# A two-layer backbone on one core: the order of one step's loads, of a gate and of some norms, two free PSUM banks, and a merged store

## The chip, the cores and the metric

The kernel runs on one core of one Trainium2 chip. A core has five engines that run side by side and wait for each other through semaphores: TensorE (PE in the profile, its weight loads PEld), VectorE (DVE), ScalarE (ACT), GpSimd (POOL) and SyncE (SP), which here only issues DMA transfers. Matmul results land in PSUM, which has eight banks; everything else lives in SBUF or in the chip's memory. The metric is the device time of one execution in microseconds; lower is better.

## The reference

Two layers work on 512 latent tokens and 256 context tokens of width 1024. Layer 0 is a bidirectional gated DeltaNet with 16 value heads, layer 1 is attention with 8 query heads, 2 key heads and an axial rotary. Each layer ends in a gate (SiLU) and an output projection, and the output is an RMS norm of the latent stream.

```python
def step(s, xs):                                   # layer 0, one chunk of 64 tokens
    qk_i, qd_i, kd_i, u_i, w_i, gl_i = xs
    v_new = u_i - jnp.einsum('bhcd,bhde->bhce', w_i, s)
    o = jnp.einsum('bhcd,bhde->bhce', qd_i, s) + jnp.einsum('bhcs,bhse->bhce', qk_i, v_new)
    s = s * gl_i[..., None, None] + jnp.einsum('bhcd,bhce->bhde', kd_i, v_new)
    return s, o

def finish(o, z):                                  # layer 0, after both directions
    o = rms_norm(jnp.transpose(o, (0, 2, 1, 3)), o_norm_g)
    return (o.reshape(b, l, DN_VAL_DIM) * jax.nn.silu(z)) @ w_out

def gqa_attend(q, k, v):                           # layer 1, q and k normed and rotated
    s = jnp.einsum('bqhgd,bkhd->bhgqk', qg, k).astype(F32) * (d ** -0.5)
    p = jax.nn.softmax(s, axis=-1)
    return jnp.einsum('bhgqk,bkhd->bqhgd', p, v).reshape(b, lq, hq, d)

h_lat = h_lat + gate[:, None] * y_lat              # each layer
return rms_norm(h_lat, final_norm_g)               # the end
```

## The kernel before

Tokens lie in six tiles of 128 rows: tiles 0 and 1 hold the context, 2 to 5 the latents. A tile pairs a chunk of 64 tokens from the front with one from the back, so that the forward and the backward direction are worked at once, one in each half of the partitions. Large products are made in three passes (`PASS`: high times high, high times low, low times high), for which operands are split into a high part, a cast by ScalarE, and a low part, a subtraction by VectorE or GpSimd.

**Up to 537 us** the projections, convolutions and the chunk matrices of layer 0 are computed, in an order that a planner in the code writes out; keys, queries, values, T (the inverted triangle) and QK of each tile are stored to memory. The last products of this part are `pp` and `pw` (L837, L861), the last store is that of T of tile 5 (L852).

**The recurrence (L1761 to L1800)** has 12 steps of 4 groups, `x` from 0 to 47, in a loop `for x in range(50)` with a pipeline of three stages: `products(x)` (state times keys and queries into `ks`, L1562; VectorE's `r`, L1565; ScalarE's `o`, L1568; GpSimd's scaling of the state, L1571, and on a second visit its sum O + o, L1574), `solve(x-1)` (T times r into `pr_all` or `pq_all`, L1588; its copy `vn`, L1590; the scaled copy `vd`, L1598 or L1600) and `update(x-2)` (QK times vn, L1614; keys times vd into `su`, L1622; VectorE's additions to O, L1628, and to the state, L1634 and L1636). Step 0 starts from a zero state and skips `products`. The two PSUM tiles `pr_all` and `pq_all` alternate with x; one half takes the solve, the other the QK product, so the solve of a group waits until the addition (L1628) of the group two before it has read its tile.

`load_step(s)` issues the loads of a step when its first group begins: key `ck` and query `cq` (L1534), two halves of the values `cv` (L1010), T (L1002), QK (L1003) and the turned key `ckt` (L1004), all on SyncE's queue. A queue issues in order; a load whose buffer is still in use holds all behind it.

At the end of the recurrence the output part of layer 0 starts for its first heads: `out_scale` (ScalarE), `out_turn` (transposes into `pt`, L1699), `out_gated` (VectorE, L1708), `out_cast` (the high half, ScalarE, L1715), `out_rest` (the low half, VectorE, L1721), then `out_product` (L1742). This order is written by hand for TensorE, VectorE, ScalarE and GpSimd.

**Layer 1** is written by hand too. Before the loop over `u` (32 pairs of a head and a tile, four more turns to drain) keys and the first queries are normed and rotated: `k_rotated` (L2086, L2087, GpSimd's sum L2088), `k_turned`, `q_cosines` and `q_sines` (L2172 to L2180), and `q_norm_steps` (L2192 to L2200), eleven small VectorE instructions of Newton steps, of which `some(norms, n)` runs the next n. In step u: `scores(u)` (L2233) into `s3`, `maxima(u)` (L2239, L2241), the exponential in `powers(u)` (ScalarE, L2248), transposes of step u-2 (L2261), products with the values (L2282) into the left half of the bank `po`, and up to u = 23 a piece of the query and gate projections (L2162, L2213). The maxima lie in `spare`, the right half of that bank. From u = 26 on `out_block` (L2296) fills the place of the pieces.

**The tail** takes the last projection of tiles 2 and 3 in chunks of columns (`CHUNKS`): tile 3 has one of 512 and two of 256, of which the last two lie in the two halves of `po`. `finish_part` (L2448 to L2450) gates a chunk, adds it and squares it, `finish_norm` takes the root, and `send` stores each half of a tile by a DMA of its own (L2471).

Of the kernel before, what the change touches and what calls it, by code (L numbers as in the profile page):

```python
# [12 lines left out]
ALU = mybir.AluOpType  # L13
# [4 lines left out]
P = 128  # L18
# [68 lines left out]
def backbone(tc, a, out):  # L87
    nc = tc.nc
    V, S, G, T = nc.vector, nc.scalar, nc.gpsimd, nc.tensor
    dma = nc.sync.dma_start  # L90
# [1039 lines left out]
    last = {}  # L1130
# [373 lines left out]
    if True:  # L1504
# [11 lines left out]
        def load_step(s):  # L1516
            nm = f"_{s}"
            t, visit = where(s)
            if s == 0:
                (Tt, QK, kt), v = opening["m"], opening["v"]  # L1520
                loads[s] = (None, kt, v, Tt, QK)
                return
            if s % 2:
                Tt = ch.tile([P, VH, 64], F32, tag="T", name="cT" + nm, bufs=1)
                v = ch.tile([P, VH, P], F32, tag="v", name="cv" + nm, bufs=1)
                QK = ch.tile([P, VH, 64], F32, tag="QK", name="cQK" + nm, bufs=1)
                kt = ch.tile([P, QH, P], F32, tag="kt", name="ckt" + nm, bufs=1)
            k0 = ch.tile([P, QH, P], F32, tag="kq0", name="ck" + nm, bufs=1) if s % 2 else by_key_heads(even_tile(s, "k"))
            if not s % 2:
                Tt, QK = even_tile(s, "T"), even_tile(s, "QK")  # L1530
                kt, v = by_key_heads(even_tile(s, "kt")), values_tile(s)
            kq = [k0, ch.tile([P, QH, P], F32, tag="kq1", name="cq" + nm)]
            for w, src in enumerate((k_d, q_d)):
                dma(kq[w], src[t])  # L1534
            values_loaded(t, v)
            mark[0] = matrices_loaded(t, visit, Tt, QK, kt)
            loads[s] = (kq, kt, v, Tt, QK)


# [37 lines left out]
        def solve(x):  # L1577

            s, p = divmod(x, 4)
            t, visit = where(s)  # L1580
            Tt = loads[s][3]
            r, = live[x]
            pr_ = prq[x % 2][:, :, 0:2]
            for i in range(2):
                for j in range(2):
                    for hf in range(2):
                        r0, o0 = hf * 64, (hf ^ j) * 64
                        T.matmul(pr_[o0:o0 + 64, j, i], Tt[r0:r0 + 64, 4 * p + 2 * j + i, :], r[r0:r0 + 64, 2 * j + i], start=True, stop=True)  # L1588
            vn = ch.tile([P, 4, P], F32, tag="vn", name=f"vn{x}", bufs=2)
            (V.tensor_copy if x == 0 else S.copy)(vn.rearrange("p (j i) d -> p j i d", j=2), pr_)  # L1590
            vd = None
            if s < 11:
                vd = ch.tile([P, 4, P], F32, tag="vd", name=f"vd{x}", bufs=2)
                for c in range(4):
                    h = 4 * p + c
                    el = (elX if c > 1 else elV)[:, visit, t, h:h + 1]
                    if s == 0 and p < 2:
                        V.tensor_scalar(vd[:, c], vn[:, c], el, None, ALU.mult)  # L1598
                    else:
                        S.activation(vd[:, c], vn[:, c], AF.Copy, scale=el)  # L1600
            live[x] = [vn, vd]
# [151 lines left out]
    AB, C = (0, 1), (2,)  # L1753
    squares = [(t, h) for t in (1, 0, 5) for h in range(VH)]
    for x in range(50):
        if x < 48:
            products(x)
        if x == 45:
            out_scale(0, AB)
        if x == 46:  # L1760
            out_scale(0, C)  # L1761
        if 0 <= x - 1 < 48:
            solve(x - 1)
        if x == 47:
            out_gated(0)
            out_cast(0)
            out_rest(0)
        if 0 <= x - 2 < 48:
            update(x - 2)
        if x == 45:  # L1770
            psU_c.__exit__(None, None, None)
            psV_c = tc.tile_pool(name="psV", bufs=2, space=PSUM, reuse_waits="tile")
            turning["p"] = psV_c.__enter__()
        if 14 <= x < 30 or x >= 35:
            for t, h in squares[:2]:
                square_o(t, h)
            del squares[:2]
        if x == 1:
            V.tensor_tensor(or2, rq, rq, ALU.mult)
        if 30 <= x < 42:  # L1780
            some(ctx_chain, (2, 4, 1, 1, 1, 1, 1, 1, 1, 1, 1, 99)[x - 30])
        if x in (43, 44, 45):
            some(chain, (3, 7, 99)[x - 43])
        if x in (28, 32, 36, 40):
            with tc.issue_after(mark[0]):
                (out_load if x < 36 else gate_load)((x - 28) // 4 % 2)
        if x in (44, 45):
            out_high(x - 44)
        if x == 46:
            out_low(0)  # L1790
            out_turn(0)
        if x == 47:
            out_low(1)
            out_load(2)
        if x == 48:
            out_scale(1)
            out_product(0, 0)
            out_turn(1)
# [436 lines left out]
    def maxima(u):  # L2235
        hq, t = divmod(u, 4)
        b = u % 2
        top = spare[:, b:b + 1]
        V.tensor_reduce(top, s3[:, b], AX.X, ALU.max, negate=True)  # L2239
        nm_ = at.tile([P, 1], F32, tag="nm", name=f"nm{u}")  # L2240
        V.tensor_tensor(nm_, top, qTs["s", hq // 2][:, t, hq % 2:hq % 2 + 1], ALU.mult)  # L2241
        return nm_
# [77 lines left out]
    some(norms, 5)  # L2320
    q2 = q_cosines(0, 2)
    q_sines(0, 2, q2)
    some(norms, 99)
    z_products(1, range(4))
    q_turned(0, 1, qo)
    k_turned(4, kr.pop(4))
    kr[5] = k_rotated(5)
    z_products(1, range(4, 8))
    q_turned(0, 2, q2)
    kv_values(lat)  # L2330
# [22 lines left out]
    for u in range(32 + 4):  # L2353
# [12 lines left out]
        elif last and u % 2 == 0:  # L2366
            z_tanh(last[1])
        if u == 0:
            q_sines(*last[1:], o)
            norms = q_norm_steps(0, spare[:, 16:48], 3, 4)  # L2370
        if turning:
            turn(u - 2, ps)
            turned(u - 2, ps)
        nm_ = maxima(u) if u < 32 else None
        if o is not None and u:
            q_sines(*last[1:], o)
        if turning:
            turned_lo(u - 2, ps)
# [3 lines left out]
            powers(u, nm_)  # L2382
        if u % 8 == 6 and u < 24:
            norms = q_norm_steps(u // 8 + 1, pg[0][:, 256:288], 0, 4)
        if u % 8 in (6, 7) or u == 0:
            some(norms, 7 if u % 8 == 6 else 99)
        for half in range(2):
            if piece and piece[0] is q_products:
# [42 lines left out]
    gated(15)  # L2431


    acc = [pg, acc1, [tr_tile(f"pso2{nh}").rearrange("p a b -> p (a b)") for nh in range(2)], [s_all[:, 1024:1536], po]]

    jks = [f2.tile([P, D], F32, tag="jko", name=f"jko{t}") for t in range(2)]
    CHUNKS = [((0, 512), (512, 512))] * 3 + [((0, 512), (512, 256), (768, 256))]

    def out_chunk(k, t, c0, n):
        cc_, (bank, b0) = slice(c0, c0 + n), divmod(c0, 512)  # L2440
        for x, (i, j) in enumerate(PASS):
            T.matmul(acc[t][bank][:, b0:b0 + n], yT[i][:, k, t * P:(t + 1) * P], wo[j][:, k, cc_], start=k == 0 and x == 0, stop=k == KT - 1 and x == 2)

    def finish_part(t, i):
        c0, n = CHUNKS[t][i]
        c, (bank, b0) = slice(c0, c0 + n), divmod(c0, 512)
        jk = jks[t]
        V.tensor_tensor(jk[:, c], acc[t][bank][:, b0:b0 + n], gate1[:, 0, c], ALU.mult)  # L2448
        V.tensor_tensor(hs[t][:, c], hs[t][:, c], jk[:, c], ALU.add)
# [16 lines left out]
        return y  # L2466

    def send(t, x, c, q):
        for hf in range(2):
            c_ = t if hf == 0 else 7 - t  # L2470
            q(out[0, c_ * 64:c_ * 64 + 64, c], x[hf * 64:hf * 64 + 64, c])  # L2471
# [99 lines left out]
```

## Time and profile before

| what | value |
|---|---|
| median of 3 runs | 1148.21 us (1148.09 to 1150.12) |
| the profiled execution | 1148.87 us |
| its span, first to last instruction | 1147.0 us |
| mean granted TensorE clock | 0.995 |
| ScalarE busy | 749.1 us (65%) |
| VectorE busy | 787.8 us (69%) |
| GpSimd busy | 600.9 us (52%) |

Times in the profile are microseconds from the start of the span. An engine's busy time is counted by instruction; an engine that is idle waits for a semaphore, and the profile names the engine, line and tile whose end came last before it went on. TensorE's matmuls are pipelined, so the rows of two neighbours overlap, and an end of a group is a little later than the start of the next. "SPq" and "ACTq" are the sequencers that issue DMA transfers; the row of an issue says nothing of when the data is there, for which the list of DMA issues has a landing time.

### The profile page before, as it was taken

The page shows a single profiled execution, that of the slowest core. Times are in us where ns is not written, and L with a number is a line of the kernel's source. Part 1 is how long each engine was busy: PE and PEld are TensorE (multiplying, and loading weights), DVE is VectorE, ACT ScalarE, POOL GpSimd, SP SyncE. Part 2 cuts the span into 40 slices and gives each one's busy share as a digit, 9 for nine tenths or more (in the row PEclk, how much of TensorE's full clock was granted, in tenths as well). Part 3 has the DMA queues.
Part 4 walks back from the last instruction along what each step waited for, and adds up shares of the span by engine and source line. Part 5 has one row for each costly group of instructions (what it writes and reads, how often), then busy time and mean ns, then how long its engine had stood idle before and what let it go on. Part 6 is the DMA issues. An engine that isn't in the chain of part 4 may idle for free.

```text
span 1147.0 us, 27235 instructions
## 1 busy us (share of the span) xinstructions
PE 1108.2 (97%) x10511; PEld 904.6 (79%) x10511; DVE 787.8 (69%) x1628; ACT 749.1 (65%) x1998; POOL 600.9 (52%) x521
## 2 busy tenths in 40 slices
PE   5999999999999999998999999999999999999996
PEld 2777788888888888887566665888787889999885
DVE  4786656688899978783688877355546476667646
ACT  4554554477877888675789888875767356666731
POOL 0554111239999999940675688556645253130900
PEclk9999999999999999999999999999999999999999
DMA  9589744765748886756998983686844112001323
GB/s 367 199 287 326 261 143 130 226 178 166 232 128 241 264 246 205 207 181 193 291 258 244 276 252 101 196 224 184 239 136 138 55 57 63 30 19 56 111 74 92
DMA packets 117138, 208.69 MB, mean 182 GB/s; under 512 B 12145, under 2 KB 76818, under 8 KB 111762
## 3 DMA queue, kind: packets, MB, share of 16 engines
q1 hardware_dynamic: 97074, 195.32, 55.2%
q10 hardware_dynamic: 19936, 11.64, 3.4%
q8 instruction: 83, 1.36, 0.5%
q14 instruction: 45, 0.37, 0.1%
HBM read 166.16 MB, written 40.67 MB: 180 GB/s over the span
## 4 chain that ended last, share of the span: by engine, by line
PE 89%; DVE 3%; issue 2%; DMA 2%; ACT 2%; POOL 1%; SPq 0%; POOLq 0%; ACTq 0%; DVEq 0%
PE g_v L926 12%; PE g_z L926 12%; PE po L1742 9%; PE ks L1562 7%; PE g_k L500 6%; PE g_q L926 6%; PE pg L2162 4%; PE su L1622 3%; PE pg L2213 3%; PE po L2282 3%; PE s L2233 3%; PE kv L2044 2%; PE pa L316 2%; PE pt L2261 2%; PE pq_all L1588 1%
## 5 line engine op out<-in xcount | busy, mean ns | idle before, releaser
L1742 PE MATMUL po<-woh,y 128*128 128x512 f32 x384 | 129.2, 401 | 0.0
L1571 POOL TENSOR_TENSOR S<-S,glb 128x512 f32<-128x512 f32 x80 | 81.9, 1045 | 82.3 <-PE ks L1562 82.1
L1680 POOL TENSOR_TENSOR wol<-wo,woh 128x1024 fp32r<-128x1024 f32 x32 | 77.5, 2422 | 55.9 <-ACT woh L1673 54.2
L810 POOL TENSOR_TENSOR X<-X,tmp 128x62 f32<-128x62 f32 (+15 forms) x93 | 98.6, 1060 | 7.3
L809 POOL TENSOR_TENSOR tmp<-L,X 128x62 f32<-128x62 f32 (+15 forms) x93 | 91.9, 989 | 6.7
L926 PE MATMUL g_z<-uh,wh_z 128*128 128x512 f32 (+1 forms) x256 | 88.6, 346 | 0.0
L926 PE MATMUL g_v<-uh,wh_v 128*128 128x512 f32 (+1 forms) x256 | 88.0, 344 | 0.0
L941 DVE SCALAR_TENSOR_TENSOR acc_v<-g_v,cwv,acc_v 128x510 f32<-128x510 f32 (+3 forms) x128 | 77.7, 614 | 14.5 <-ACT acc_v L933 11.0
L926 PE MATMUL g_z<-ul,wh_z 128*128 128x512 f32 (+1 forms) x256 | 86.9, 339 | 0.4 <-issue 0.4
L926 PE MATMUL g_z<-uh,wl_z 128*128 128x512 f32 (+1 forms) x256 | 86.6, 338 | 0.0
L926 PE MATMUL g_v<-ul,wh_v 128*128 128x512 f32 (+1 forms) x256 | 86.1, 336 | 0.0
L926 PE MATMUL g_v<-uh,wl_v 128*128 128x512 f32 (+1 forms) x256 | 86.1, 336 | 0.0
L1742 PEld LDWEIGHTS po<-woh,y 128*128 128x128 f32 x384 | 72.3, 188 | 15.4 <-issue 0.3
L1742 PE MATMUL po<-wol,y 128*128 128x512 f32 x192 | 75.4, 393 | 0.0
L1636 DVE TENSOR_TENSOR S<-su,S 128x512 f32<-128x512 f32 x80 | 51.5, 686 | 8.1 <-PE su L1622 6.5
L1708 DVE SCALAR_TENSOR_TENSOR pt<-pt,og,z 128x128 f32<-128x128 f32 x96 | 34.4, 358 | 32.5 <-PE pt L1699 30.2
L555 POOL TENSOR_TENSOR kt<-kt,kss 128x768 f32<-128x768 f32 x8 | 11.6, 1472 | 85.6 <-DVE kss L183 57.1
L1562 PE MATMUL ks<-S,ck 128*64 128x256 f32 x352 | 55.4, 392 | 1.0 <-ACT O L1568 1.0
L1565 DVE SCALAR_TENSOR_TENSOR r<-ks,negV,cv 128x128 f32<-128x128 f32 x176 | 52.3, 344 | 5.2 <-PE ks L1562 2.2
L1562 PE MATMUL ks<-S,cq 128*64 128x256 f32 x352 | 53.6, 379 | 0.0
L926 PEld LDWEIGHTS g_z<-ul,wh_z 128*128 128x128 f32 x256 | 49.0, 191 | 5.4 <-issue 0.6
L926 PEld LDWEIGHTS g_z<-uh,wl_z 128*128 128x128 f32 x256 | 48.9, 191 | 5.4
(463 smaller groups left out, 3341.6 us busy)
## 6 DMA issues: line engine op xcount, KB each, us to landing
aw<-in_ada_late SPq DMA_DIRECT2D x16, 1024.0 KB, 7.3
wo<-in_dn_w_out SPq DMA_DIRECT2D x32, 512.0 KB, 3.7
cv<-v_d SPq DMA_DIRECT2D x22, 512.0 KB, 8.7
aw<-in_ada_first SPq DMA_DIRECT2D x8, 1024.0 KB, 11.6
w_z<-in_dn_w_in SPq DMA_DIRECT2D x16, 512.0 KB, 5.0
w_v<-in_dn_w_in SPq DMA_DIRECT2D x16, 512.0 KB, 4.5
v_d<-vt ACTq DMA_DIRECT2D x16, 384.0 KB, 4.2
cT<-t_d SPq DMA_DIRECT2D x12, 512.0 KB, 9.4
```

Source lines behind the costliest of these rows:

```text
L500: T.matmul(kbank[h, i][:, :n], w[:, k], u[:, k, c0:c0 + n], start=k == 0 and n_ == 0, stop=k == KT - 1 and n_ == len(passes) - 1)
L809: G.tensor_tensor(tv, bcast(L[:, :, j + 1:, j], 3, j + 1), bcast(X[:, :, j, 0:j + 1], 2, n), ALU.mult)
L810: G.tensor_tensor(X[:, :, j + 1:, 0:j + 1], X[:, :, j + 1:, 0:j + 1], tv, ALU.subtract)
L926: T.matmul(ps[:, :m], w[:, k], u[:, k, c0:c0 + m], start=k == 0 and n_ == 0, stop=k == KT - 1 and n_ == 2)
L941: V.scalar_tensor_tensor(acc[:, c0 + lo:c0 + hi], ps[:, lo + j - 2:hi + j - 2], cwv[:, j, ct:ct + 1], acc[:, c0 + lo:c0 + hi], ALU.mult, A ...
L1562: T.matmul(ks[r0:r0 + 64, w], kq[w][:, hh, r0:r0 + 64], St[hh][:, d], start=True, stop=True)
L1565: V.scalar_tensor_tensor(r[:, 2 * j + i], ks[:, 0, i], negV[:, visit, t, h:h + 1], v[:, h], ALU.mult, ALU.add)
L1571: G.tensor_tensor(St[hh], St[hh], bcast(g_, 3, P), ALU.mult)
L1636: V.tensor_tensor(St[hh], sj, St[hh], ALU.add)
L1680: G.tensor_tensor(wl, raws.pop(n), halves[n][0], ALU.subtract)
L1742: T.matmul(acc[nh], y[i][:, j, :], ww[k][:, nh * 512:(nh + 1) * 512], start=h == 0 and x == 0, stop=h == VH - 1 and x == 2)
L2162: T.matmul(q_bank(p, t), uL[i][:, k, t * P:(t + 1) * P], wq[j][:, k], start=k == 0 and n_ == 0, stop=k == KT - 1 and n_ == 2)
```

## The change

Seven places change.

1. `load_step`: in step 1 the query is loaded behind values, T and QK, ahead of the turned key. Other steps keep their order.
2. `solve`: in step 0 the scaled copies `vd` of groups 2 and 3 are made by GpSimd, two instructions of two heads each, in place of four on ScalarE.
3. The loop of the recurrence, at x = 47: `out_gated(0)` and `out_cast(0)` stand ahead of `products(47)`, `out_rest(0)` behind `update(45)`; before, all three stood between `solve(46)` and `update(45)`.
4. `maxima`: in steps 24 and 25 the result lies in `pg[0]`, a bank that no product uses in those steps, in place of `spare`.
5. Ahead of the loop over u, the last Newton steps stand behind `k_turned(4)` and `k_rotated(5)`.
6. In the loop, at u = 0, `q_sines` stands behind `maxima(0)` as in other steps, and the Newton steps of the last query tile run at u = 1 in place of u = 0.
7. The tail: the last chunk of tile 3 lies in `pg[0]`, and tile 3, whose two halves are neighbours in the output, is stored by one DMA for each column half in place of two.

```diff
             kq = [k0, ch.tile([P, QH, P], F32, tag="kq1", name="cq" + nm)]
-            for w, src in enumerate((k_d, q_d)):
-                dma(kq[w], src[t])
+            dma(kq[0], k_d[t])
+            if s > 1:
+                dma(kq[1], q_d[t])
             values_loaded(t, v)
-            mark[0] = matrices_loaded(t, visit, Tt, QK, kt)
+            dma(Tt, t_d[t, :, visit])
+            dma(QK, qk_d[t, :, visit])
+            if s == 1:
+                dma(kq[1], q_d[t])
+            mark[0] = dma(kt, kt_d[t]).ins
...
-                    if s == 0 and p < 2:
+                    if s == 0 and p > 1:
+                        if c % 2 == 0:
+                            G.tensor_tensor(vd[:, c:c + 2], vn[:, c:c + 2], bcast((elX if c > 1 else elV)[:, visit, t, h:h + 2], 2, P), ALU.mult)
+                    elif s == 0:
                         V.tensor_scalar(vd[:, c], vn[:, c], el, None, ALU.mult)
...
     for x in range(50):
+        if x == 47:
+            out_gated(0)
+            out_cast(0)
         if x < 48:
             products(x)
...
             solve(x - 1)
-        if x == 47:
-            out_gated(0)
-            out_cast(0)
-            out_rest(0)
         if 0 <= x - 2 < 48:
             update(x - 2)
+        if x == 47:
+            out_rest(0)
...
-        top = spare[:, b:b + 1]
+        top = (pg[0] if u in (24, 25) else spare)[:, b:b + 1]
...
-    some(norms, 99)
     z_products(1, range(4))
     q_turned(0, 1, qo)
     k_turned(4, kr.pop(4))
     kr[5] = k_rotated(5)
+    some(norms, 99)
     z_products(1, range(4, 8))
...
         if u == 0:
-            q_sines(*last[1:], o)
             norms = q_norm_steps(0, spare[:, 16:48], 3, 4)
...
-        if o is not None and u:
+        if o is not None:
             q_sines(*last[1:], o)
...
-        if u % 8 in (6, 7) or u == 0:
+        if u % 8 in (6, 7) or u == 1:
             some(norms, 7 if u % 8 == 6 else 99)
...
-    acc = [pg, acc1, [tr_tile(f"pso2{nh}").rearrange("p a b -> p (a b)") for nh in range(2)], [s_all[:, 1024:1536], po]]
+    acc = [pg, acc1, [tr_tile(f"pso2{nh}").rearrange("p a b -> p (a b)") for nh in range(2)], [s_all[:, 1024:1536], po, pg[0]]]
...
+    def place(t, c0):
+        return (2, 0) if t == 3 and c0 == 768 else divmod(c0, 512)
...
     def send(t, x, c, q):
+        if t == 3:
+            q(out[0, 192:320, c], x[:, c])
+            return
         for hf in range(2):
```

More of the change, by code (lines that the diff above doesn't have):

```diff
@@ L2431, in backbone @@
     gated(15)
-    acc = [pg, acc1, [tr_tile(f"pso2{nh}").rearrange("p a b -> p (a b)") for nh in range(2)], [s_all[:, 1024:1536], po]]
+    acc = [pg, acc1, [tr_tile(f"pso2{nh}").rearrange("p a b -> p (a b)") for nh in range(2)], [s_all[:, 1024:1536], po, pg[0]]]
     jks = [f2.tile([P, D], F32, tag="jko", name=f"jko{t}") for t in range(2)]
     CHUNKS = [((0, 512), (512, 512))] * 3 + [((0, 512), (512, 256), (768, 256))]
+    def place(t, c0):
+        return (2, 0) if t == 3 and c0 == 768 else divmod(c0, 512)
     def out_chunk(k, t, c0, n):
-        cc_, (bank, b0) = slice(c0, c0 + n), divmod(c0, 512)
+        cc_, (bank, b0) = slice(c0, c0 + n), place(t, c0)
         for x, (i, j) in enumerate(PASS):
@@ L2445, in finish_part @@
         c0, n = CHUNKS[t][i]
-        c, (bank, b0) = slice(c0, c0 + n), divmod(c0, 512)
+        c, (bank, b0) = slice(c0, c0 + n), place(t, c0)
         jk = jks[t]
```

## The prediction

> **What bounds the kernel now.** I read the page first, then the waits of TensorE alone, then, at each wait that the change touches, the timeline and the chain of waits. The page:
>
> ```profile
> span 1147.0 us, 27235 instructions
> PE 1108.2 (97%) x10511; PEld 904.6 (79%) x10511; DVE 787.8 (69%) x1628; ACT 749.1 (65%) x1998; POOL 600.9 (52%) x521
> ```
>
> TensorE is busy 97% of the span, and the change takes no matmul away. 1147.0 - 1108.2 leaves 38.8 us, so it can gain only where TensorE waits and at the two ends. The list of TensorE's waits has six that the change touches, none above 2.5 us; each is shown below. Between them TensorE is full, as a window of the recurrence shows (us, then busy us of TensorE, its weight loads, VectorE, ScalarE, POOL, each with its count, then granted clock, DMA share, GB/s):
>
> ```profile
> 553.00:644.00 91.00, 91.00 (x1540) 58.87 (x1536) 73.88 (x168) 80.05 (x276) 59.30 (x56) 1.00 0.93 261
> ```
>
> So a microsecond won at one place arrives at the end. The DMA engines are at 0.93 there, but loads are issued as TensorE frees buffers, so an earlier TensorE also means earlier loads.
>
> **Part 1: step 1's loads.** From the timeline (start, us, engine, line, operation; in brackets the idle time before it and what ended it); the sixth row is from SyncE's waits (us, times, longest):
>
> ```profile
> 526.25 0.33 SPq L1534 DMA_DIRECT2D ck<-k_d  x1
> 534.85 0.32 SPq L1534 DMA_DIRECT2D cq<-q_d  x1
> 535.22 2.37 SPq L1010 DMA_DIRECT2D cv<-v_d  x2
> 543.65 1.29 DVE L1634 COPY S<-su 128x512 f32<-128x512 f32 x2 [1.31 <-PE su L1622]
> 546.93 0.61 DVE L1565 SCALAR_TENSOR_TENSOR r<-ks,negV,cv 128x128 f32<-128x128 f32 x2 [1.99 <-DMA cv<-v_d]
> SPq L1534 <- PE pw L861: 8.2, 1, 8.2
> 543.99 0.60 PE L1562 MATMUL ks<-S,cq 128*64 128x256 f32 x4
> 548.31 0.65 PE L1562 MATMUL ks<-S,ck 128*64 128x256 f32 x4 [0.96 <-ACT O L1568]
> 551.08 0.67 PE L1588 MATMUL pr_all<-r,cT 64*64 64x128 f32 x16 [0.83 <-ACT O L1626]
> ```
>
> The query load (cq) waits 8.2 us for the last `pw` product, with values, T and QK behind it in SyncE's queue. The values come so late that r starts at 546.93, though VectorE was free at 543.65 + 1.29 = 544.94. With the query behind them, the three can go out right after the key, from 526.6 on. Then r starts 1.99 earlier, and what follows it on ScalarE does too. What is late next is TensorE itself: without the 0.96, the second ks group starts at 547.35; it takes 1.94 (548.31 to 551.08 - 0.83) and ends at 549.29, when the copy that pr_all waits for is done since 551.08 - 1.99 = 549.09. Both waits go: 0.96 + 0.83 = **1.8 us**.
>
> The new risk is the query, used at 543.99 and now behind 2 MB. The load on the DMA engines, the two ends of the old order (landing time at the end of the row) and ScalarE's 1 MB store of T:
>
> ```profile
> 525.00:535.00 10.00, 9.81 (x254) 7.99 (x255) 0.69 (x1) 4.14 (x8) 0.00 (x0) 0.83 0.62 214
> 535.00:545.00 10.00, 9.03 (x150) 6.89 (x150) 5.31 (x15) 6.01 (x13) 0.26 (x1) 1.00 0.87 267
> cq<-q_d SPq DMA_DIRECT2D x1, 512.0 KB, 3.9
> cQK<-qk_d SPq DMA_DIRECT2D x1, 512.0 KB, 12.8
> 537.18 0.34 ACTq L852 DMA_DIRECT2D t_d<-Tt  x1
> ```
>
> From 525 to 535 the queues moved 10 x 214 = 2.14 MB; the moved loads add 2.0, the query 0.5: 4.64 MB, which at 267 GB/s are through at 525 + 17.4 = 542.4, in time. If the whole store of 537.18 goes first, 1 MB or 3.8 us come on top: 546.2, and TensorE waits 2.2. I take "in time", since the values can start eight microseconds sooner, and keep 1.8 - 2.2 = -0.4 to 1.8 as bounds. [...]
>
> In step 0, groups 2 and 3 now scale vd on POOL, in two instructions for ScalarE's four. The trace has none such; the nearest has its size (ns, shortest, median, longest), and POOL is idle until its first scaling of S:
>
> ```profile
> L2088 POOL TENSOR_TENSOR kr<-kr,tmk x4: 732/735/741, 911.2 to 925.7; 128x256 f32<-128x256 f32 x4
> 544.74 2.04 POOL L1571 TENSOR_TENSOR S<-S,glb 128x512 f32<-128x512 f32 x2 [42.72 <-PE ks L1562]
> ```
>
> 2 x 0.735 = 1.5 us. Group 3 follows that scaling and its own vn (near 547.3), so it is ready near 548.8; its su comes after pr_all and the QK product, near 550.3. **0 us**, covered by those 1.5; if the cover were gone, at most 1.5 lost, and nothing gained, as ScalarE is not late there.
>
> **Part 2: the first head gated ahead.** The end of the recurrence:
>
> ```profile
> 710.64 0.33 PE L1699 MATMUL pt<-ident,so 128*128 128x128 f32 x1 [0.32 <-ACT so L1692]
> 712.03 0.61 DVE L1565 SCALAR_TENSOR_TENSOR r<-ks,negV,cv 128x128 f32<-128x128 f32 x2 [1.22 <-PE ks L1562]
> 713.26 0.62 PE L1614 MATMUL pq_all<-vn,cQK 64*64 64x128 f32 x16
> 713.42 1.14 DVE L1708 SCALAR_TENSOR_TENSOR pt<-pt,og,z 128x128 f32<-128x128 f32 x3
> 715.59 0.68 DVE L1628 TENSOR_TENSOR O<-pq_all,O 128x512 f32<-128x512 f32 x1
> 716.32 0.67 PE L1588 MATMUL pq_all<-r,cT 64*64 64x128 f32 x16 [2.44 <-DVE O L1628]
> ```
>
> TensorE waits 2.44 for the addition of group 45 (L1628), which VectorE does behind the gating (1.14), the wait for ScalarE's cast and the low half. The change puts gating and cast before the products of group 47, the low half behind the addition. The gating can start at 710.64 + 0.33 = 710.97, ends near 712.15 in VectorE's idle 1.22, and delays r by 0.1. The addition then waits for its product only, 713.26 + 0.62 and 0.1 of passage: 714.0 in place of 715.59, **1.6 us**. The low half follows at 714.7, before the first projection can start (near 715.8). Bounds: 1.0 (r and ScalarE's o pushed by the cast) to 2.4.
>
> **Part 3: norms.** TensorE's wait for the rotation of key 5, the last Newton step that stands before it, and the first steps of the attention loop:
>
> ```profile
> 923.63 0.17 DVE L2200 SCALAR_TENSOR_TENSOR sq<-kv,qy 128x6 f32<-128x6 f32 x1
> 926.45 0.44 PE L2070 MATMUL kt<-ident,kr 128*128 128x128 f32 x2 [0.34 <-POOL kr L2088]
> 932.60 1.33 PE L2233 MATMUL s<-kT,qT 128*128 128x512 f32 x6 [0.25 <-ACT pr L2248]
> 932.66 0.15 DVE L2192 TENSOR_SCALAR po<-sq 128x2 f32<-128x2 f32 x1
> 934.64 0.16 DVE L2200 SCALAR_TENSOR_TENSOR sq<-po,qy 128x2 f32<-128x2 f32 x1
> 937.19 0.19 ACT L2248 ACTIVATION_READ_ACCUMULATOR pr<-s,nm,sq 128x1 f32 x1
> 937.43 1.31 PE L2233 MATMUL s<-kT,qT 128*128 128x512 f32 x6 [0.75 <-ACT pr L2248]
> ```
>
> Six steps of 0.2 us, the last at 923.63, move behind that rotation: 1.2 earlier, and the 0.34 goes, **0.3 us** (0 to 0.34). At u = 0 the sines (two instructions, some 0.8) move behind the first maxima, and eleven steps, 932.66 to 934.80, behind the second exponential. Scores of step u start 0.05 after the exponential of u-1 is read out (937.19 + 0.19 = 937.38, 937.43). Both exponentials come earlier, by 0.8 and about 1.3, more than the waits: 0.25 + 0.75 = **1.0 us** (0.25 to 1.0). Late next are the third maxima, pushed by the moved steps to some 938.3; their exponential would end near 940.6, before TensorE is through its 2.9 us of query products.
>
> **Part 4: maxima of steps 24 and 25 in a free bank.** The value products no longer wait for them:
>
> ```profile
> 1064.08 1.32 PE L2282 MATMUL po<-pT,vv 128*128 128x256 f32 x9 [0.93 <-DVE nm L2241]
> 1064.95 0.19 ACT L2248 ACTIVATION_READ_ACCUMULATOR pr<-s,nm,sq 128x1 f32 x1
> 1067.77 1.32 PE L2282 MATMUL po<-pT,vv 128*128 128x256 f32 x9 [0.60 <-DVE nm L2241]
> 1068.65 0.19 ACT L2248 ACTIVATION_READ_ACCUMULATOR pr<-s,nm,sq 128x1 f32 x1
> ```
>
> The waits sum to 1.53. But the order seen in part 3 is late next: the scores follow the exponential. Exponential 24 is read out at 1065.14, so scores 25 start at 1065.19 at the earliest; now the value products end at 1065.40. That wins 0.2, and 0.2 again one step later (1068.89 against 1069.09): **0.4 us**, bounds 0 and 1.5.
>
> **Part 5: the tail.**
>
> ```profile
> 1130.39 5.83 PE L2442 MATMUL po<-wo,yT 128*128 128x256 f32 x48
> 1136.26 0.42 DVE L2448 TENSOR_TENSOR jko<-po,gate 128x256 f32<-128x256 f32 x1 [2.39 <-PE po L2442]
> 1137.85 0.41 DVE L2448 TENSOR_TENSOR jko<-po,gate 128x256 f32<-128x256 f32 x1
> L2471 ACTq DMA_DIRECT2D out<-hg x2: 562/584/605, 1142.2 to 1142.8; - x2
> ```
>
> The second chunk is complete after 24 of the 48 matmuls, near 1133.4, but its reading waits for all, as the third lies in its bank. With the third elsewhere, the second's work is over by 1135.6, and the third's starts at 1136.26 in place of 1137.85: **1.6 us**, all on the last chain (1.4 if a semaphore adds 0.2). Two stores per queue become one: at most one issue, 0.58, at least 0, as the bytes stay; I take **0.4 us**, nearer to the issue.
>
> **Sum.** 1.8 + 0 + 1.6 + 0.3 + 1.0 + 0.4 + 1.6 + 0.4 = 7.1 us. The profiled execution took 1148.87 (span 1147.0 and 1.87 around it), so 1141.8 by its own time. It lies 0.66 above the median of the three runs, 1148.21; from that I forecast **1141.1**.
>
> **Rivals.**
>
> (a) At steps 24 and 25 nothing is late behind the maxima: 1.5 in place of 0.4, 1140.0. For it: both rows name nm alone. Against it: the exponentials end only 0.2 before the scores. [...]
>
> (b) The query lands at 546.2: part 1 gives -0.4, 1143.3. For it: DMA shares of 0.87 to 0.93. Against it: the 0.62 before 535 leaves room.
>
> (c) Part 2 doesn't do what it says, since the gating waits longer for head 0's last transpose and pushes r and o as far as it was pushed itself: 1.6 lost, 1142.7. Against it: 1.22 us idle.
>
> (d) Slower: values, T and QK are held by the same `pw`. Then they go out from 534.8 on and the query some 4 us later, in QK's old place, whose 12.8 us bring it to about 552: the query products wait 8 us from 543.99, and part 1's 1.8 drowns in that. The granted clock need not hold through such a hole: 525 to 535 ran at 0.83, 1.7 us lost, and I count as much again. 1148.2 + 8 + 1.7 - 5.3 (the other parts) = 1152.6. It decides from 549.3 on, when the wait passes 5.3. Against it: the key, of the same line, went out at 526.25, and SyncE's wait for `pw` is listed once.
>
> **How the numbers follow.** Forecast 0.58, (a) 0.12, (b) 0.16, (c) 0.04, (d) 0.10. Of (d), 0.04 goes to a query near 549, within 0.2% (2.3 us, about what a measurement tells from no change), 0.06 to slower; all else, 0.90, is faster. The range runs from 1138.8 ((a) with part 2 at 2.4 and the store at 0.58) to 1145.2 ((b) with parts 2 and 3 at their lower bounds and no gain by the store); outside lie (d) and corners.
>
> **What would show it.** Right: values issued before 530 and no ks wait at 548; no 2.4 us wait on pq_all; no wait of scores at u = 1 and 2; at steps 24 and 25 scores that wait for pr in place of products that wait for nm; the first reading of the second chunk near 1133.9. Wrong: ks waiting for cq; values issued behind 534.8; new idle of TensorE in the window that is full now.

## The result, and the profile after

| | before | after |
|---|---|---|
| median | 1149.24 us (6 runs, 1148.09 to 1152.77) | 1143.2 us (6 runs, 1140.86 to 1146.6) |
| ratio | | 0.9935, 95% interval 0.9915 to 0.9956 |
| the profiled execution | 1148.87 us | 1143.75 us |

The change is faster by 6.0 us, inside the range (1138.8 to 1145.2) and 2.1 above the forecast of 1141.1. The sum of the terms was 7.1 us; by the two profiled executions it came to 5.1. This section shows where the difference lies, the experiments why.

The page of the changed kernel, and its list of TensorE's waits (us in total, times, longest):

```profile
span 1141.8 us, 27230 instructions
PE 1107.7 (97%) x10511; PEld 904.8 (79%) x10511; DVE 790.3 (69%) x1628; ACT 747.1 (65%) x1990; POOL 602.1 (53%) x525
```

```profile
PE g_z L926 <- issue: 3.2, 3, 2.2
PE pp L837 <- issue: 1.9, 1, 1.9
PE s L2242 <- ACT pr L2257: 1.4, 2, 0.8
PE su L1630 <- issue: 1.3, 2, 1.1
PE pq_all L1593 <- DVE O L1636: 0.9, 1, 0.9
```

TensorE's idle time went from 38.8 to 1141.8 - 1107.7 = 34.1 us. Gone from the list are the waits of ks and pr_all in step 1, of po for nm, of kt, and of the scores at u = 1 and 2; pq_all waits 0.9 in place of 2.4. New are the waits of the scores for pr at steps 25 and 26 (part 4; before, scores waited for it at u = 1 and 2), 0.3 of ks for the query, and 3.2 us of g_z, a projection of layer 0, for "issue", which means that the trace names nothing that it waits for. Before the change that last entry was 0.4.

The two traces can be laid side by side by the starts of the same instructions. The third column is after minus before, the last what the stretch ending there won or lost:

| up to | before | after | difference | of this stretch |
|---|---|---|---|---|
| pw of tile 5 | 533.48 | 534.50 | +1.02 | +1.02 |
| first pr_all of the recurrence | 537.76 | 541.21 | +3.45 | **+2.43** |
| second product with r of step 1 | 554.86 | 556.88 | +2.02 | **-1.43** |
| ks of group 47 | 710.90 | 712.13 | +1.23 | -0.79 |
| the pq_all behind it that waits for O | 716.32 | 716.03 | -0.29 | **-1.52** |
| the qt ahead of key 5 | 921.06 | 920.53 | -0.53 | -0.24 |
| scores of step 2 | 937.43 | 934.86 | -2.57 | **-2.04** |
| scores of step 24 | 1061.26 | 1058.86 | -2.40 | +0.17 |
| scores of step 26 | 1068.93 | 1066.27 | -2.66 | **-0.26** |
| hg's first half, last tile | 1133.12 | 1130.49 | -2.63 | +0.03 |
| end of the span | 1147.0 | 1141.8 | -5.2 | **-2.57** |

All five parts won something where they stand. Stretches without an edit differ by up to 1.0 us as well, and those of equal kernels do too: in two traces of the kernel with part 1 undone the first pr_all comes at 536.19 and at 539.20. The loss is ahead of them: 1.0 us in code that no edit touches, and 2.4 between the last pw and the first pr_all, where the only edit is that 2 MB of loads go out earlier. The timeline of that stretch (start, us, engine, line, operation, idle time before it), the two loads, and the query's use:

```profile
527.90 2.99 SPq L1010 DMA_DIRECT2D cv<-v_d  x2
535.86 0.32 SPq L1540 DMA_DIRECT2D cq<-q_d  x1
538.62 0.39 PE L926 MATMUL g_z<-ul,wh_z 128*128 128x256 f32 x1 [2.17 <-issue]
547.89 0.44 PE L1567 MATMUL ks<-S,cq 128*64 128x256 f32 x2 [0.28 <-DMA cq<-q_d]
```

The values went out at 527.90, before the wait for pw, as the prediction had it. The query landed 12.0 us after its issue, at 547.86, not at 542.4; it delays TensorE by 0.28 only because TensorE itself is 3.45 late.

The other places, in the order of time (the row of scores at u = 1 and 2 stands without a wait):

```profile
716.03 0.67 PE L1593 MATMUL pq_all<-r,cT 64*64 64x128 f32 x16 [0.91 <-DVE O L1636]
930.86 0.38 PE L2079 MATMUL qt<-ident,qr 128*128 128x128 f32 x2
930.99 1.30 PE L2242 MATMUL s<-kT,qT 128*128 128x512 f32 x6
934.86 1.21 PE L2242 MATMUL s<-kT,qT 128*128 128x512 f32 x6
1062.59 1.31 PE L2242 MATMUL s<-kT,qT 128*128 128x512 f32 x6 [0.79 <-ACT pr L2257]
1066.27 1.33 PE L2242 MATMUL s<-kT,qT 128*128 128x512 f32 x6 [0.65 <-ACT pr L2257]
1131.16 0.41 DVE L2459 TENSOR_TENSOR jko<-po,gate 128x256 f32<-128x256 f32 x1
1133.63 0.42 DVE L2459 TENSOR_TENSOR jko<-pg,gate 128x256 f32<-128x256 f32 x1 [0.81 <-PE pg L2453]
1137.28 0.72 ACT L2539 ACTIVATE hg<-hg,fr 128x512 f32<-128x512 f32 x1 [2.23 <-DVE fr L2476]
1137.72 0.34 SPq L2481 DMA_DIRECT2D out<-hg  x1
1138.04 0.34 ACTq L2481 DMA_DIRECT2D out<-hg  x1
```

In the tail the second chunk is read at 1131.16, 2.5 us ahead of the third; with the third in its own bank neither waits for the other's matmuls.

### The profile page after: what moved, and what is told of

Read it like the earlier page. It is cut to its first block, busy times and chain, and to the rows that moved or that the text cites. A ratio compares the mean times of both kernels' runs of the same rounds, so it can differ in the third digit from the quotient of the medians.

```text
span 1141.8 us, 27230 instructions
## 1 busy us (share of the span) xinstructions
PE 1107.7 (97%) x10511; PEld 904.8 (79%) x10511; DVE 790.3 (69%) x1628; ACT 747.1 (65%) x1990; POOL 602.1 (53%) x525
## 3 DMA queue, kind: packets, MB, share of 16 engines
q8 instruction: 83, 1.36, 0.5%
## 5 line engine op out<-in xcount | busy, mean ns | idle before, releaser
L810 POOL TENSOR_TENSOR X<-X,tmp 128x62 f32<-128x62 f32 (+15 forms) x93 | 101.3, 1089 | 7.3
L809 POOL TENSOR_TENSOR tmp<-L,X 128x62 f32<-128x62 f32 (+15 forms) x93 | 89.1, 958 | 6.7
```

What stands on the lines that cost most here:

```text
L809: G.tensor_tensor(tv, bcast(L[:, :, j + 1:, j], 3, j + 1), bcast(X[:, :, j, 0:j + 1], 2, n), ALU.mult)
L810: G.tensor_tensor(X[:, :, j + 1:, 0:j + 1], X[:, :, j + 1:, 0:j + 1], tv, ALU.subtract)
```

## The experiments

Two theories of the 2.4 us stood at the start. A: TensorE's program itself comes by DMA, in packets that the trace lists as queue q8 of kind "instruction" (83 packets, 1.36 MB, in the traces of both kernels), and the moved loads delay it. B: such waits are chance, of the kind that spreads equal runs over 5 us.

### 1. The old load order, all else changed

```diff
-            dma(kq[0], k_d[t])
...
+            for w, src in enumerate((k_d, q_d)):
+                dma(kq[w], src[t])
             values_loaded(t, v)
+            mark[0] = matrices_loaded(t, visit, Tt, QK, kt)
```

> The changed kernel with step 1's loads in the old order (key, query, values, T, QK, transposed keys); all else as changed. In the changed kernel's trace the recurrence began at 541.21, 3.45 us later than before, though no edit touches TensorE's order there; 2.17 of it is one wait in g_z at 536.46 that nothing in the trace releases ('issue'). Theory A (the moved 2 MB delay the packets that bring TensorE's program, queue q8 of kind instruction): no such wait between 530 and 541, pr_all begins some 2.2 us earlier; the stage from the first pr_all to the ks of group 6 takes 15.2 us again, with 0.96 and 0.83 on ks and pr_all, in place of 13.8. Net 0.8 us faster than the changed kernel: some 1142.4, ratio to before 0.994. Theory B (the wait is chance, of the kind that spreads equal runs over 5 us): the wait comes or not whatever the order; the mean loses the 1.4 us of the stage and nothing comes back: 1144.6, ratio 0.996. Both theories: the first ks with the query does not wait.

Measured: 1143.2 us median (6 runs), ratio 0.9942 (0.9928 to 0.9957). No wait in g_z, as theory A had it, and the first pr_all starts at 538.17, 3.0 earlier than in the changed kernel. But the stage did not go back to its old length: from the first pr_all to the second product with r it takes 15.5, against 17.1 before and 15.7 after (the expectations count to the ks ahead of that product, 1.9 less). The row of r says why:

```profile
545.68 1.13 DVE L1565 SCALAR_TENSOR_TENSOR r<-ks,negV,cv 128x128 f32<-128x128 f32 x4 [0.32 <-DMA cv<-v_d]
```

In the same order as before, r waits 0.32 for the values in place of 1.99; they landed 7.4 us behind the first pr_all, in the trace of before 9.0. So the wait that part 1 removes is not a fixed price.

### 2. Only the values ahead

```diff
             values_loaded(t, v)
-            dma(Tt, t_d[t, :, visit])
-            dma(QK, qk_d[t, :, visit])
             if s == 1:
                 dma(kq[1], q_d[t])
+            dma(Tt, t_d[t, :, visit])
+            dma(QK, qk_d[t, :, visit])
```

> The changed kernel with only the values moved ahead of step 1's query: key, values, query, T, QK, transposed keys. 1 MB in place of 2 MB goes out before the query can. Theory A (moved bytes delay TensorE's program): the wait in g_z at 536 is gone or under 1 us, as half the bytes come before 535; the values still land before r needs them, so the stage from the first pr_all to the ks of group 6 keeps its 13.8 us; the query goes out near 535 and lands before 544, so the 0.28 us wait of ks for it goes too. 2.2 + 0.3 us faster than the changed kernel: 1140.7, ratio to before 0.992. T and QK then land as before the change, near 548, used from 551 on. Theory B (chance): no difference from the changed kernel but for the 0.28: 1142.9, ratio 0.994. If T or QK come too late here, pr_all of the third ks group waits for a DMA, and the stage is longer than 13.8.

Measured: 1142.56 us median (6 runs), ratio 0.9934 (0.9918 to 0.9951), the number that both theories allow within the interval. The trace sides with A: no wait in g_z, none for the query or T, and the stage takes 15.2.

### 3. Parts 2 and 4 and the merged store undone

```diff
-        if x == 47:
-            out_gated(0)
-            out_cast(0)
         if x < 48:
             products(x)
...
-        top = (pg[0] if u in (24, 25) else spare)[:, b:b + 1]
+        top = spare[:, b:b + 1]
...
-        if t == 3:
-            q(out[0, 192:320, c], x[:, c])
-            return
```

> The changed kernel with three edits undone, which lie 350 us and 70 us apart: the first head's gating and cast stand behind the products of group 47 again, the maxima of steps 24 and 25 in the spare half of po again, the last token tile stored in two halves again. Expected, each from its own rows: (1) the wait of the last pq_all for O is 2.4 again in place of 0.91, 1.5 us; (2) products wait for nm by 0.93 and 0.60 and scores no longer for pr; what steps 24 to 26 take is 0.2 us longer (my forecast of the change said 0.4, the rival 1.5); (3) two stores on each queue; from the last hg to the end of the span 5.5 us as before in place of 4.5 (forecast: 0.4, bound 0.58). Theory A of the load order (moved bytes delay TensorE's program): a wait of about 2 us in g_z between 530 and 541 is there again, as the loads are the changed ones; chance theory: present or absent at random.

Measured: one run, 1148.04 us. The wait in g_z is there, 1.09. The wait for O is 2.44 again; but the table of stages shows more than that wait. Two windows of this kernel and the first of them of the kernel before (us, busy us of TensorE, its weight loads, VectorE, ScalarE, POOL, granted clock, DMA share, GB/s):

```profile
716.00:723.00 7.00, 5.12 (x58) 3.79 (x58) 1.97 (x4) 3.93 (x10) 5.30 (x3) 0.76 0.61 179
723.00:730.00 7.00, 7.00 (x36) 5.79 (x33) 3.87 (x9) 4.95 (x23) 2.49 (x2) 1.00 0.44 133
```

```profile
716.00:723.00 7.00, 6.68 (x73) 5.31 (x73) 3.18 (x7) 4.36 (x14) 4.28 (x2) 1.00 0.52 155
```

Here the granted clock falls to 0.76 behind the wait, and from 712.46 to 722.38 the stage takes 3.08 us longer than in the changed kernel (712.13 to 718.97): 1.52 for the wait, 1.56 for the clock. In the first trace of before the same wait was followed by 1.00. Steps 24 to 26 take 0.21 longer. From the last hg to the end of the span 5.3 us (1140.86 to 1146.2) in place of 4.5, with this in between (the changed kernel's issues took 0.34 each):

```profile
1141.29 1.11 SPq L2481 DMA_DIRECT2D out<-hg  x2
1141.61 1.21 ACTq L2481 DMA_DIRECT2D out<-hg  x2
```

1.11 - 0.34 and 1.21 - 0.34: the second store of a queue costs 0.8 to 0.9 at the end, not the 0.58 that I took for the upper bound.

### 4. Part 3, the third bank and POOL's vd undone

```diff
-                    if s == 0 and p > 1:
+                    if s == 0 and p < 2:
...
     kr[5] = k_rotated(5)
-    some(norms, 99)
...
-        if u % 8 in (6, 7) or u == 1:
+        if u % 8 in (6, 7) or u == 0:
...
-        return (2, 0) if t == 3 and c0 == 768 else divmod(c0, 512)
+        return divmod(c0, 512)
```

> The changed kernel with three other edits undone: the norm steps stand where they stood (six in front of key 5's rotation; sines of query tile 3 before the first maxima and eleven steps behind the first exponential), the third chunk of the last token tile lies in po beside the second again, and ScalarE scales vd of groups 2 and 3 again in place of POOL. Expected: (1) from the kv products at 878 to the scores of step 3 it takes 2.0 us longer than in the changed kernel, though the waits that the list of waits then shows sum to 1.3 (0.34, 0.25, 0.75): TensorE's matmul records overlap, so a wait costs more than the idle time beside it; if the idle time is the price, 1.3; (2) the first reading of the second chunk waits for all 48 matmuls, 1.6 us more on the last chain; (3) POOL against ScalarE for vd: no change in the stage from the first pr_all to the ks of group 6 (13.8), if my 0 was right; 15.2 if the POOL scaling and not the values' load made the gain there. Theory A of the load order: a wait of about 2 us in g_z between 530 and 541 again.

Measured: one run, 1144.52 us. The wait in g_z is there, 1.35. The stage of step 1 takes 15.2 with ScalarE's vd, so POOL's part is worth nothing, as forecast. From the kv products to the scores of step 3 it takes 2.4 us longer than the changed kernel (forecast 2.0). The waits around the start of the loop, as listed and as rows:

```profile
PE s L2239 <- ACT pr L2254: 1.2, 2, 1.0
PE kt L2076 <- POOL kr L2094: 0.3, 1, 0.3
```

```profile
928.68 0.38 PE L2076 MATMUL qt<-ident,qr 128*128 128x128 f32 x2
929.31 1.32 PE L2239 MATMUL s<-kT,qT 128*128 128x512 f32 x6 [0.24 <-ACT pr L2254]
```

The list sums to 1.5; the stage lost 2.4. (In the kernel before: 1.3 and 2.2.) The rows show where the rest is: qt starts at 928.68 and is held to be busy for 0.38, so the scores at 929.31 seem to wait 0.24. In the changed kernel, where nothing is late, the scores follow the same qt after 0.13 (930.86 to 930.99). The wait costs 929.31 - 928.68 - 0.13 = 0.50. In the tail, the second chunk is read at 1132.97, behind all 48 matmuls, and the last chain ends 1.58 later, as forecast (1.6).

### 5. The last pp products further back

All traces so far have a wait of 1.8 to 2.2 us within pp, where 128 products of pw and 128 of pp, all 32x32, stand in a row. If theory A is right, it is the same wait.

```diff
+            if n == N - 1 and i == 0:
+                half = last["half"] = Piece("PE", 2.74, t0, gemm_part, n, i, range(4), after=[wh, wl, last["g", n - 1]], takes=["g"], holds=[("wh", wh)], lands=0.2, slack=0.0)
+                g.append(Piece("PE", 2.74, t0, gemm_part, n, i, range(4, KT), after=[half], holds=[("wh", wh), ("g", half)], lands=0.2, slack=0.0))
+                continue
...
-        pp = Piece("PE", 1.23, -20, j_first, t, after=U, slack=soon, takes=["gq"], holds=[(u, U[0]), ("mo", mo_of[t])], lands=0.1)
+        pp = Piece("PE", 1.23, -20, j_first, t, after=U + ([last["half"]] if t == 5 else []), slack=0.0 if t == 5 else soon, takes=["gq"], holds=[(u, U[0]), ("mo", mo_of[t])], lands=0.1)
```

> The kernel with only the values ahead, and one more edit: the last pp products (tile 5), which stand right behind the last pw products of tile 4, are put behind the first twelve of the 24 g_z matmuls that follow them; no other engine's work changes, but for ScalarE's copies of U, two of which now stand ahead of pn. Theory A (TensorE's program arrives in 16 KB blocks by DMA, and 256 products of 32x32 in 2.4 us use it up faster than it comes): the wait of 1.8 to 2.2 us within pp, which all six traces so far have, goes or falls below 0.5, since 2.7 us of long matmuls now lie between the bursts; with it goes the granted clock of 0.57 to 0.67 in the 4 us behind it, which costs another 1.7 us. 3.5 to 3.9 us faster than the kernel with values ahead: some 1138.8, ratio to before 0.990. Rival: the wait is for something else that the trace does not name (the transposed U, a semaphore): it goes with pp to its new place and keeps its 2 us, and the time stays at 1142.6, ratio 0.9934.

Measured: 1143.0 us median (6 runs), ratio 0.9941 (0.9925 to 0.9958). The forecast of 1138.8 was missed, but the trace is the most useful one. The wait in pp is gone, so the rival falls, and the clock behind it stays at 1.00; but g_z now waits 5.04. Its list of waits between 500 and 562:

```profile
PE g_z L928 <- issue: 5.0, 1, 5.0
```

The packets of q8 tell the same. Each is 16 KB. The first two columns are the starts of two that follow each other, worked out from the trace's list of packets:

| kernel | block | next | apart | wait in g_z |
|---|---|---|---|---|
| before, first and second trace | 526.30, 526.09 | 532.03, 531.42 | 5.7, 5.3 | 0, 0 |
| old loads | 526.91 | 532.50 | 5.6 | 0 |
| part 1 undone, two traces | 526.16, 527.73 | 531.12, 533.41 | 5.0, 5.7 | 0, 0 |
| after, first and second trace | 527.28, 527.29 | 535.65, 533.16 | 8.4, 5.9 | 2.17, 0 |
| experiments 3 and 4 (2 MB ahead) | 527.61, 528.25 | 535.08, 534.92 | 7.5, 6.7 | 1.09, 1.35 |
| values ahead, without and with the split | 528.27, 528.33 | 534.33, 535.95 | 6.1, 7.6 | 0, 5.04 |
| old loads with the split | 526.97 | 532.53 | 5.6 | 2.37 |

A view of the changed kernel's transfers in two windows, 528.3 to 535.5 and 535.6 to 537.0, shows the same: no packet of q8 in the first, with the queues at 103% of the 16 engines; one in the second (columns: packets, MB, share). Before the change the queues were about as full, 97.5% from 528.0 to 531.9, but then came down, to 19% from 532 to 533, and the block came at 532.03: what the moved loads change is how long the queues stay full.

```profile
q1 hardware_dynamic: 309, 1.75, 78.4%
q10 hardware_dynamic: 144, 0.39, 24.4%
q14 instruction: 1, 0.01, 0.3%
```

```profile
q1 hardware_dynamic: 54, 0.32, 104.0%
q8 instruction: 1, 0.02, 6.0%
```

In the twelve traces there are 44 waits for "issue" of over 0.4 us, and all 44 end 1.2 to 1.6 us behind the end of a packet of q8. A count says more: a trace has 83 such packets and about 21,320 records of TensorE (matmuls, weight loads and its sequencer's), which is 257 a packet. The records that waited lie multiples of 256 apart, in the first trace of before at 7874, 9922 and 15298. Numbered from the first, the record that waited is 194 beyond a multiple of 256 in 37 cases and 193 in the other 7, and the packet that it waited for is each time the one that is due by this count. So I read these waits: TensorE has run out of program. The trace itself names no cause.

### 6. Part 1 undone whole, and both kernels once more

```diff
+            for w, src in enumerate((k_d, q_d)):
+                dma(kq[w], src[t])
...
-                    if s == 0 and p > 1:
+                    if s == 0 and p < 2:
```

> The changed kernel without its first part: step 1's loads in the old order, and ScalarE scaling vd of groups 2 and 3; all else as changed. In the run with the old loads alone undone, the values landed 7.4 us behind the first pr_all, in the run before 9.0 us, and the wait of r fell from 1.99 to 0.32. Theory B (when the values land varies by a microsecond or more from run to run, so that the old order costs between 0.3 and 1.8): the r wait lies anywhere from 0.3 to 2.0, and first pr_all to first product with r takes 11.6 to 13.4. Theory C (POOL's vd is what made the difference): r waits 2.0 and the stage takes 13.3 again, as before. Both: no wait in g_z at 536, since the moved loads are not there; the time then equals that of the changed kernel within 0.1%, ratio to before 0.994, as what the stage loses (0.3 to 1.8) the missing g_z wait gives back (1.1 to 2.2).

Measured: 1142.28 us median (6 runs), ratio 0.9934 (0.9917 to 0.9951). No wait in g_z, as forecast. r waits 0.16, with the old order and ScalarE's vd:

```profile
543.53 1.13 DVE L1565 SCALAR_TENSOR_TENSOR r<-ks,negV,cv 128x128 f32<-128x128 f32 x4 [0.16 <-DMA cv<-v_d]
```

So theory C falls, and the price of the old order does vary.

> The changed kernel once more, for a second trace and times on this chip. If the g_z wait belongs to the moved loads (theory A), it is there a fourth time, 1.1 to 2.2 us; if it is chance, it may be missing. Ratio to before 0.9935 as in the first comparison.

Measured: 1142.95 us median (6 runs, 1141.65 to 1149.27), ratio 0.9945 (0.9924 to 0.9965). The profiled execution was the longest, and the wait in g_z, expected a fourth time, is missing: the block came at 533.16. What came in its place is rival (b), with a loss of clock that I had priced for (d) alone:

```profile
535.72 0.32 SPq L1540 DMA_DIRECT2D cq<-q_d  x1
548.19 1.12 PE L1567 MATMUL ks<-S,cq 128*64 128x256 f32 x4 [1.98 <-DMA cq<-q_d]
```

```profile
545.00:549.00 4.00, 2.02 (x14) 0.89 (x16) 1.29 (x2) 0.00 (x0) 0.00 (x0) 0.81 0.38 149
549.00:553.00 4.00, 4.00 (x46) 2.71 (x46) 1.22 (x4) 1.73 (x6) 2.14 (x3) 0.50 0.78 258
```

TensorE reached the query 1.4 us earlier than in the first trace (548.19 - 1.98 = 546.21, there 547.61), and the query landed at 548.1, 12.4 us after its issue. TensorE waits 1.98 and then runs at half its clock. From the first pr_all to the second product with r it takes 21.5 us, 5.8 more than in the first trace.

> The kernel before once more, for a second trace. No wait in g_z at 536 (theory A); the wait for O on the last pq_all is 2.4 again; when the values of step 1 land against the first pr_all shows how much the old order varies (9.0 us in the first trace; theory B: 7.4 to 9; theory C: 9.0). Whether the granted clock falls behind the 2.4 us wait at 716, as it did to 0.76 with the first head's gating put back, and did not in the first trace, is open.

Measured: one run, 1151.94 us. No wait in g_z. The stage of step 1 takes 16.7 (17.1 in the first trace), the wait for O is 2.45, and this time the clock fell behind it:

```profile
716.00:723.00 7.00, 5.17 (x58) 4.03 (x58) 1.92 (x4) 3.88 (x10) 4.82 (x3) 0.76 0.55 179
```

In step 1, r waits 1.59 here, until 8.8 us behind the first pr_all:

```profile
546.30 1.13 DVE L1565 SCALAR_TENSOR_TENSOR r<-ks,negV,cv 128x128 f32<-128x128 f32 x4 [1.59 <-PE pr_all L1614]
```

The product that the row names is of the group before, and with part 1 undone r ran ahead of that product (543.53 against 544.30), so r does not depend on it. The values are the likely cause, as in the first trace; their second half has no landing time in this trace.

### 7. The split with the old load order

The edits are those of experiments 5 and 6 together, and the second kernel is that of experiment 6 again, for a comparison on one chip.

> The changed kernel without its first part, and with the last pp products behind twelve of the g_z matmuls. With the values ahead this split took the 2.1 us wait out of pp, but a wait of 5.0 came in g_z at 538.86: the block of TensorE's program behind it came at 535.95, 7.6 us after the block before it, where in traces with the old load order blocks follow each other there after 5 to 5.6. Theory A (blocks come late while bulk loads run, and TensorE waits until 1.2 to 1.6 us behind the block's end): with the old loads nothing bulky but the key and a store of T goes out in these microseconds, so the block comes near 532 to 533.5 and the wait in g_z is 0 to 1.5; the pp wait and the low clock behind it are gone, pr_all begins 2 to 3.5 us earlier than without the split, time 1139 to 1140.5, ratio to before 0.991 to 0.992, to the kernel without part 1 0.997 to 0.998. Rival (the block comes a set time after the one before it, whatever the load): a wait of some 4 to 5 in g_z again, and no gain.

> The changed kernel without its first part once more, beside the split on the same chip. Ratio to before 0.9934 as the first time, if the load order is worth nothing in the mean; the wait in pp 1.8 to 2.2. In the first trace the granted clock stayed at 1.00 behind that wait, where seven other traces fell to about 0.6 there; which of the two comes is open, and it is worth 1.7 us.

Measured: 1141.58 us (6 runs, 1138.95 to 1144.38), ratio 0.9934 (0.9911 to 0.9957), against 1142.93 (8 runs, 1139.72 to 1146.19), ratio 0.9947 (0.9923 to 0.997). The intervals overlap widely; a gain of the split isn't shown. Its wait in g_z:

```profile
PE g_z L928 <- issue: 2.4, 1, 2.4
```

The wait is 2.4 with the old loads and 5.0 with 1 MB more ahead, at the same place of the same order. These are one trace each, and the two traces of the changed kernel differ by as much (2.17 and 0); the table says more. In all six traces of the old order the two blocks lie 5.0 to 5.7 apart, in all six with more loads ahead 5.9 to 8.4. So the loads delay the block, as theory A says, by an amount that varies, and the rival (a set time after the block before) falls. But 0 to 1.5 was too low, and the first pr_all comes at 538.47, no earlier than without the split (536.19 and 539.20): TensorE comes there earlier than the program, so the split moves the wait of pp rather than ending it, and the clock behind g_z falls in its turn (0.57 from 534 to 538). In the second kernel it fell behind pp again (0.58 from 527 to 531).

## Why the prediction was right, and where it was not

**The time** was right to 0.2%, with parts that were wrong in both directions; that they nearly cancel is luck. The range should have run from 1139.0 to 1145.4 by its own terms, 0.2 higher at both ends, which changes nothing.

**Part 1, 1.8 forecast, nothing in the mean.** Two steps failed. The first is "4.64 MB, which at 267 GB/s are through at 525 + 17.4 = 542.4, in time": the query landed at 547.86 and 548.1 in the two traces of the change, later than rival (b)'s 546.2, and at 546.3 and 546.1 in experiments 3 and 4. The sum counted bytes from 525 on, as if the queues could start with all of it; but the query can go out only at 535.7 to 536.1 (it waits for pw in both orders), and once issued it needs 12.0 and 12.4 us (10.2 in experiments 3 and 4), much like QK, the last of the old order (12.8). That figure stood in a quoted row, and I used it for rival (d) only. In the first of these traces QK, ahead of the query in the queue, landed at 544.7, 3.2 before it.

Second, nothing in the prediction asked what else moves over these engines: the 16 KB blocks that I take for TensorE's program came up to 2.7 us later, and g_z waited 1.1 to 2.2 in three of the four traces with the changed order. In the fourth the program came in time, and so TensorE met the late query.

The stage did win its 1.43, but what it removes was not a fixed price either: r waits 1.99 and 1.59 in the two traces of the kernel before, and 0 to 0.32 in the four other traces of the old order, in two of which it waits 2.0 and 1.7 for the values of step 2 instead. The waits of TensorE behind r are 1.8 and 1.4, then 1.1, 0.8 and twice none. Up to group 47 the kernel without part 1 is the same program as the kernel before, so no other edit explains this spread; what sets it stays open. The sign that the prediction names for its own error, ks waiting for cq, stands in both traces of the change. On one chip the kernel without part 1 took 1142.28 and the changed one 1142.95. Over all runs, on several chips, the means are 1142.5 (14 runs) and 1143.7 (12), 1.2 apart with an interval of 1.7 either way: a gain of 1.8 is out, and that part 1 is a little worse is not shown.

**POOL's vd, 0 forecast**: right; with ScalarE in its place the stage takes the same 15.2.

**Part 2, 1.6 forecast, 1.5 by the waits**: right in mechanism and size, and rival (c) fell: r starts 1.17 behind the ks of group 47, before 1.13. But in two of three traces with the long wait the granted clock fell behind it, worth another 1.56. This belongs to the gain in the mean and was in no term.

**Part 3, 0.3 + 1.0 forecast, 2.0 measured (2.4 when undone)**: the mechanism was right, the size was not. I took the idle time beside a wait for its price. TensorE's records overlap by up to 0.25 us when nothing is late (930.86 + 0.38 against 930.99), so a wait costs that much more than its idle time shows; three waits make the 0.7.

**Part 4, 0.4 forecast, 0.2 measured**: scores wait for pr and no longer products for nm, so the rival (a) with 1.5 fell. "That wins 0.2, and 0.2 again one step later" counted one gain twice: a step lasts from one exponential to the next and takes 3.68 us now (1062.59 to 1066.27) and 3.69 before (1065.24 to 1068.93), so the second 0.2 is the first, passed on.

**Part 5, 1.6 + 0.4 forecast, 1.6 + 0.8 to 0.9 measured**: the bank was exact. The store's bound of 0.58 was the duration of one issue; two issues in a row took 1.11 and 1.21 in place of 0.34.

**The sum.** With these sizes: 0 + 1.5 + 2.0 + 0.2 + 1.6 + 0.9 = 6.2, and up to 1.0 more by the clock (1.56 in two of three). Measured: 6.0 in the first comparison, 1149.36 - 1142.95 = 6.4 in the second; without part 1 7.1 and 7.2. The forecast also started from a median of three runs, 1148.21, where six runs gave 1149.24.

No kernel tried is faster than the changed one by more than its interval. Best guess for the order of loads, by the traces: the old one or only the values ahead, both of which avoid the late query.

## What to carry to other kernels

Before a load is moved to an earlier place, take the landing time that the last one in that burst had, not bytes over bandwidth (here 12.8 us, which 12.0 and 12.4 met, where the bytes gave 542.4 for 547.86 and 548.1), and ask what small transfers it delays: here blocks that I take for the matrix engine's own program, 5.9 to 8.4 us apart in place of 5.0 to 5.7. Price a wait by the starts of the two instructions against the same pair elsewhere (2.4 in experiment 4), not by the idle time beside it (1.5). And when a chain binds step after step, a gain at its head counts once.

## What the runs showed of the hardware

- **Waits for "issue" on TensorE** end 1.2 to 1.6 us behind a 16 KB packet of the instruction queue, and only where a block of 256 records of TensorE begins (44 of 44). In the first traces of the two kernels those over 1 us came where 256 products of 32x32 pass in 2.4 us (pp, 2.13 and 1.89, with the DMA engines at a share of 0.16 and 0.15 in the 3 us before), or where transfers fill the queues (g_z 2.17 at 1.03, su 1.35 and 1.11 at 0.98 and 1.00); two shorter ones, 0.42 and 0.85 in g_z, followed shares of 0.75 and 0.70. Equal kernels have them in other places from run to run, which may be much of the 5 us by which equal runs differ (the changed kernel's two traces: 2.17 and none in g_z, 1.11 and 2.15 in su). The longest is 5.04 us (g_z, experiment 5).
- **The granted clock** fell to 0.5 for about 3.4 or 6.8 us behind 16 of the 19 waits of TensorE of 1.8 us and more (outside the two ends of the span), and behind none of the 28 from 0.9 to 1.75. Behind pp, a window of the changed kernel and the one exception there, part 1 undone:

```profile
527.00:531.00 4.00, 4.00 (x44) 3.15 (x31) 0.00 (x0) 2.86 (x5) 0.00 (x0) 0.57 0.86 310
```

```profile
527.00:531.00 4.00, 4.00 (x19) 3.29 (x19) 0.00 (x0) 2.04 (x4) 0.00 (x0) 1.00 0.99 356
```

  0.57 over 4 us is 3.4 us at half the clock, or 1.7 us lost; 0.81, 0.50 and 0.78 in the windows from 545 to 549, 553 and 556 in the second trace of the change are 6.8. A wait near 2 us was followed by such a loss or by nothing: behind the wait for O the window from 716 to 723 shows 1.00 in the first trace of before (2.44), 0.76 in the second (2.45) and 0.76 in experiment 3 (2.44).
